# Attention of a hybrid streaming encoder on one Trainium2 core: chunks in pairs, unpadded queries, weight splits on one engine, one rescaling moved

## The chip, the cores and the metric

The kernel is one launch on one core of a Trainium2 chip. Five engines work side by side, each on its own queue of instructions: TensorE (PE in the profile) multiplies matrices into PSUM, VectorE (DVE) and ScalarE (ACT) read PSUM and SBUF, GpSimd (POOL) works on SBUF alone, and SyncE (SP) issues most of the transfers. The metric is the time of one execution on the device in microseconds, the median of several runs; lower is better.

## What is computed

The reference is one inference step of a two-layer encoder. 16 meta tokens and 256 new frames (the prompt) and 32 frames of a running stream (the sample) share all weights, so the kernel carries 304 tokens side by side. A layer is a half-step SwiGLU, a mixer and a second half-step SwiGLU, each between two RMS norms. Of the mixer this is the part that the change touches:

```python
s = jnp.einsum('bnqkgd,bnskd->bnkgqs', qb, kb).astype(jnp.float32) * ATTN_SCALE   # 64 ** -0.5
m = jnp.maximum(jnp.max(scores, axis=-1, keepdims=True), sink)
p = jnp.exp(scores - m)
return p / (jnp.sum(p, axis=-1, keepdims=True) + jnp.exp(sink - m))
```

There are 8 query heads in 2 groups, each group with one key and value head of 64 channels, and one learned sink per head. The prompt is attended in 4 chunks of 64 queries; a chunk sees up to 192 keys. The sample sees 128 cached keys and its own 32, the meta tokens see themselves. Beside the attention the mixer has 8 retention heads, a gate and an output projection.

## The kernel before

Activations lie transposed: channels on partitions, the 304 tokens along the free axis. Every large product is written by `mm3` as three products of rounded fp32 parts (L233, L234 and L236: weight high by input high, weight low by input high, weight high by input low). A weight piece of 128x512 arrives by DMA (`raw`), ACT rounds it to `hi` (L182), and a subtraction makes `lo` (L185); `split_one` does both. The pieces are split up to 8 ahead of their use. One piece feeds 12 matmuls. While a mixer's projection runs, every second subtraction goes to POOL (`POOLN = 2`), otherwise all go to DVE.

The order of the work is fixed when the program is written. `group4` and `group2` emit matmuls and call `tick`, which moves a counter on (775 for 6 matmuls of a `group2`). Side work waits in the lists `later`, `A` (attention) and `R` (retention) with a due count, and is emitted between the matmuls when the counter passes it; so it stands in each engine's queue at that place, whatever the clock says. `START`, `D_UNIT`, `D_NORM`, `D_TRANS`, `D_PV`, `KT` and `VT` are such counts: the start of a head group's attention, the distance of its units, and the offsets of normalising, transposing and of the product with the values.

The mixer computes the projection in this order: keys, values and queries of head group 0 (`group4`), queries of head group 1, then twice rotary keys, rotary queries and retention values, then two gates (`group2` each), and behind `flush` and `gate_out` the output projection in two `group4` of 8 pieces. `done_q` scales the queries with the norm's factor `rb` into `qb`. A unit of attention is one chunk of one head group: its stationary operand is 128 channels by 128 columns, in which one head of each pair fills the upper 64 rows and the other the lower 64, with zeros elsewhere, so that two matmuls (L981) give the scores of 4 heads. `softmax` reduces (L957), takes the sink in with two small operations (L958, L959), lets ACT exponentiate (L961); `norm` adds the sink's term (L966), inverts (L967) and scales on ACT (L968) and DVE (L969). Then PE transposes (L991), ACT (L999) and DVE (L997) copy out, and PE multiplies with the values (L1009). `side_unit` does the same for the sample and the meta tokens (L1032, L1033, L1030, L1042, L1056). PE transposes the scaled values once (L928, in the list under `VT`).

The residual `x` is kept multiplied by a norm's deviation after each sub-layer; `Post.unscale` undoes that, with a reciprocal on DVE (L539) and 8 products on POOL (L541). It stands in the mixer ahead of the second rotary queries and in a feed-forward layer at its third pair of output columns. `Post.done0` and `done1` take the output projection's results out of PSUM: ACT squares (L480, L493), POOL adds the squares of the first half (L483).

## Time and profile before

| | |
|---|---|
| median of 3 runs | 1239.14 us (1237.02 to 1241.27) |
| the profiled execution | 1237.22 us, its span 1235.4 us |
| granted TensorE clock, mean of the span | 0.987 |
| busy share of the span | PE 96%, PE weight load 93%, DVE 67%, ACT 48%, POOL 21% |
| bytes moved | 182.52 MB, 148 GB/s |

The profile was taken in one execution. Its time is 1.9 us under the median of the three runs and 1.8 us longer than its span. The two mixers lie at about 252 to 390 us and 859 to 990 us of the span. A busy share is a mean over stages with different limits.

### The profile page before, as it was taken

To read this page: it belongs to the slowest core of one execution; us is meant where nothing else is said; L and a number is where in the kernel's file an instruction comes from. 1 tells how busy PE (TensorE), PEld (TensorE's weight loads), DVE (VectorE), ACT (ScalarE), POOL (GpSimd) and SP (SyncE) were. 2 spreads that over 40 slices of the span, in tenths; PEclk is the share of its full clock that TensorE was granted. 3 is DMA by queue.
4 is the path that set the end of the run, shared out by engine and by line. 5 is a ranking of instruction groups with operands and counts; after the bars stand their busy time and mean duration, and the time that the engine had idled before them with its cause. 6 is when DMAs were issued, how large, how long until landed. Compare 5 with 4: busy or idle time off the path is not lost. (4 is left out here: it accounts for less than half of the span.)

```text
span 1235.4 us, 22814 instructions
## 1 busy us (share of the span) xinstructions
PE 1187.0 (96%) x8650; PEld 1153.7 (93%) x8650; DVE 828.3 (67%) x1501; ACT 596.2 (48%) x1226; POOL 254.1 (21%) x254
## 2 busy tenths in 40 slices
PE   8999999999999999999999999998999998999995
PEld 8999999897899999999999999998878988999995
DVE  7676654587767886564498656457875777766543
ACT  6454544455445545444355444344544553555442
POOL 4200001263625320001032000015435262000000
PEclk9999999999999999999999999999999999999998
DMA  7765455443233564554435554553533525645531
GB/s 226 164 183 159 139 190 165 157 143 111 83 109 120 154 188 144 169 181 145 148 98 176 159 176 144 183 159 122 167 96 113 154 65 175 196 147 161 193 108 39
DMA packets 155310, 182.52 MB, mean 148 GB/s; under 512 B 12016, under 2 KB 125984, under 8 KB 154944
## 3 DMA queue, kind: packets, MB, share of 16 engines
q1 hardware_dynamic: 153488, 178.84, 46.9%
q0 software_dynamic: 1344, 1.76, 1.0%
q8 instruction: 68, 1.11, 0.4%
q10 hardware_dynamic: 368, 0.47, 0.1%
q14 instruction: 42, 0.34, 0.1%
HBM read 175.70 MB, written 2.23 MB: 144 GB/s over the span
## 5 line engine op out<-in xcount | busy, mean ns | idle before, releaser
L233 PE MATMUL bk<-act,hi 128*128 128x304 f32 (+1 forms) x1824 | 559.8, 309 | 14.5 <-DVE act L516 6.5
L234 PE MATMUL bk<-act,lo 128*128 128x304 f32 (+1 forms) x1824 | 546.9, 302 | 0.6 <-DVE lo L185 0.6
L236 PE MATMUL bk<-act,hi 128*128 128x304 f32 (+1 forms) x1824 | 526.0, 303 | 4.0 <-DVE act L396 3.6
L185 DVE TENSOR_TENSOR lo<-raw,hi 128x512 fp32r<-128x512 f32 x604 | 416.0, 732 | 139.3 <-ACT hi L182 135.9
L182 ACT ACTIVATE hi<-raw 128x512 fp32r<-128x512 f32 x647 | 369.1, 621 | 148.6 <-PE bk L236 123.4
L233 PEld LDWEIGHTS bk<-act,hi 128*128 128x128 f32 x1824 | 345.9, 190 | 23.0 <-DVE act L516 8.0
L234 PEld LDWEIGHTS bk<-act,lo 128*128 128x128 f32 x1824 | 346.2, 190 | 2.1 <-DVE lo L185 1.1
L236 PEld LDWEIGHTS bk<-act,hi 128*128 128x128 f32 x1824 | 338.6, 190 | 7.2 <-DVE act L396 7.1
L233 PE MATMUL bk<-hh,hi 128*128 128x304 f32 (+1 forms) x704 | 210.4, 300 | 0.0
L234 PE MATMUL bk<-hh,lo 128*128 128x304 f32 (+1 forms) x704 | 210.1, 299 | 0.0
L236 PE MATMUL bk<-hl,hi 128*128 128x304 f32 (+1 forms) x704 | 207.9, 301 | 0.0
L483 POOL TENSOR_TENSOR acc<-acc,sq 128x304 f32<-128x304 f32 (+1 forms) x18 | 16.1, 894 | 577.7 <-ACT sq L480 576.5
L563 ACT ACTIVATE sg<-tg 128x304 f32<-128x304 f32 (+1 forms) x88 | 40.0, 455 | 192.1 <-DVE tg L562 190.8
L233 PEld LDWEIGHTS bk<-hh,hi 128*128 128x128 f32 x704 | 132.6, 188 | 0.0
L234 PEld LDWEIGHTS bk<-hh,lo 128*128 128x128 f32 x704 | 132.3, 188 | 0.0
L236 PEld LDWEIGHTS bk<-hl,hi 128*128 128x128 f32 x704 | 131.0, 188 | 0.0
L562 DVE TENSOR_TENSOR tg<-bk,rb 128x304 f32<-128x304 f32 (+1 forms) x88 | 40.9, 465 | 71.4 <-PE bk L236 71.3
L566 ACT ACTIVATE hh<-tu 128x304 fp32r<-128x304 f32 (+1 forms) x88 | 40.0, 455 | 68.8 <-DVE tu L565 68.8
L567 DVE TENSOR_TENSOR hl<-tu,hh 128x304 fp32r<-128x304 f32 (+1 forms) x88 | 41.6, 472 | 46.0 <-ACT hh L566 46.0
L185 POOL TENSOR_TENSOR lo<-raw,hi 128x512 fp32r<-128x512 f32 x44 | 59.2, 1356 | 46.4 <-ACT hi L182 46.4
L515 POOL TENSOR_TENSOR x<-x,s 128x304 f32<-128x304 f32 (+1 forms) x35 | 31.3, 927 | 130.8 <-ACT s L507 130.8
L541 POOL TENSOR_TENSOR x<-x,rs 128x304 f32<-128x304 f32 (+1 forms) x40 | 41.0, 1062 | 77.9 <-DVE rs L539 64.4
(238 smaller groups left out, 937.0 us busy)
## 6 DMA issues: line engine op xcount, KB each, us to landing
raw<-in_ffn_w_in_dram SPq DMA_DIRECT2D x352, 256.0 KB, 4.6
raw<-in_ffn_w_out_dram SPq DMA_DIRECT2D x88, 512.0 KB, 4.7
raw<-in_w_in_dram SPq DMA_DIRECT2D x36, 512.0 KB, 3.9
raw<-in_w_out_dram SPq DMA_DIRECT2D x16, 512.0 KB, 3.9
raw<-in_w_in_dram SPq DMA_DIRECT2D x16, 256.0 KB, 3.0
dec<-in_dec_dram SPq DMA_DIRECT2D x2, 1280.0 KB, 7.1
t<-t SPq DMA_DIRECT2D x24, 76.0 KB, 2.2
out_dram<-xgm SPq DMA_DIRECT2D x2, 384.0 KB, 3.5
```

The lines of the kernel that those rows point to most:

```text
L182: ACT.activation(out=hi, in_=r, func=ACTF.Copy)
L185: (POOL if i and st["pool"] and i % st["pool"] == 0 else DVE).tensor_tensor(out=lo, in0=r, in1=hi.bitcast(F32), op=ALU.subtract)
L233: PE.matmul(out=out, lhsT=a, rhs=xh, start=first, stop=False)
L234: PE.matmul(out=out, lhsT=b, rhs=xh, start=False, stop=False)
L236: PE.matmul(out=out, lhsT=a, rhs=xl, start=False, stop=last)
L483: POOL.tensor_tensor(out=self.acc[:, T0:], in0=self.acc[:, T0:], in1=sq[:, T0:], op=ALU.add)
L515: POOL.tensor_tensor(out=x[:, j, T0:], in0=x[:, j, T0:], in1=self.s[:, T0:], op=ALU.mult)
L541: POOL.tensor_tensor(out=x[:, k, T0:], in0=x[:, k, T0:], in1=rs[:, T0:], op=ALU.mult)
L562: DVE.tensor_tensor(out=tg[:, T0:], in0=bk[j][:, :n], in1=rb[:, T0:], op=ALU.mult)
L563: ACT.activation(out=sg[:, T0:], in_=tg[:, T0:], func=ACTF.Silu)
L566: ACT.activation(out=hh[a][:, T0:], in_=tu[:, T0:], func=ACTF.Copy)
L567: DVE.tensor_tensor(out=hl[a][:, T0:], in0=tu[:, T0:], in1=hh[a][:, T0:].bitcast(F32), op=ALU.subtract)
```

## The change

It does four things. (1) Queries are kept unpadded (`qa`): a head's 64 channels stand on the 64 rows of its half, scaled by -1/8, and the score matmul of each half uses 64 rows of the array, with the two halves in two PSUM banks. Two neighbouring chunks make one unit (`attn_pair`). The same holds for the sample and the meta tokens. (2) The negated sink is copied as one more column beside the scores in PSUM, so that the minimum, the exponentials and their sum take it in; the two small operations, the sink's own exponential and the addition go. (3) All subtractions of the weight splits run on DVE. (4) `unscale` of the mixer is emitted early in its output projection, and that of the feed-forward layers ahead of their output projection; the last layer keeps its place. The due counts are changed with it.

```diff
-POOLN = 2
...
-START = (12613, 11713)
-D_UNIT = 1987
-D_NORM = 1188
-D_TRANS = 3200
-D_PV = 5574
-KT = 7700
-VT = 5787
+START = (11000, 11713)
+D_UNIT = 4100
+D_NORM = 2800
+D_TRANS = 6500
+D_PV = 9300
+KT = 10500
+VT = 8500
...
+UNSCALE = 3000
...
-        (POOL if i and st["pool"] and i % st["pool"] == 0 else DVE).tensor_tensor(out=lo, in0=r, in1=hi.bitcast(F32), op=ALU.subtract)
+        DVE.tensor_tensor(out=lo, in0=r, in1=hi.bitcast(F32), op=ALU.subtract)
...
-                if g == 2 and prev:
+                if g == 2 and prev and last:
                     prev.unscale()
...
+            if prev and not last:
+                later.append((clock[0] + UNSCALE, prev.unscale))
...
-        qb = tl("qb", [P, 2, 2, 4, 2, CH])
-        qs = tl("qs", [P, 2, 2, 2, DEC])
-        POOL.memset(qb, 0.0)
-        POOL.memset(qs, 0.0)
-        qm = None
-        if not lastl:
-            qm = tl("qm", [P, 2, 2, 2, NMETA])
-            POOL.memset(qm, 0.0)
+        qa = tl("qa", [P, 2, 4, 2, CH])
...
-                for par in range(2):
-                    s = slice(64 * par, 64 * par + 64)
-                    DVE.tensor_tensor(out=qb[s, g, m, :, par], in0=y[s, NMETA - o:SA - o].rearrange("p (c t) -> p c t", c=4),
-                                      in1=rb[s, NMETA:SA].rearrange("p (c t) -> p c t", c=4), op=ALU.mult)
-                    DVE.tensor_tensor(out=qs[s, g, par, m], in0=y[s, SA - o:N - o], in1=rb[s, SA:N], op=ALU.mult)
-                    if qm is not None:
-                        DVE.tensor_tensor(out=qm[s, g, par, m], in0=y[s, 0:NMETA], in1=rb[s, 0:NMETA], op=ALU.mult)
+
+                def scaled(out, a, e):
+                    DVE.scalar_tensor_tensor(out=out, in0=y[:, a - o:e - o], scalar=-0.125, in1=rb[:, a:e], op0=ALU.mult,
+                                             op1=ALU.mult)
+                DVE.scalar_tensor_tensor(out=qa[:, g, :, m], in0=y[:, NMETA - o:SA - o].rearrange("p (c t) -> p c t", c=4),
+                                         scalar=-0.125, in1=rb[:, NMETA:SA].rearrange("p (c t) -> p c t", c=4),
+                                         op0=ALU.mult, op1=ALU.mult)
...
-        def softmax(S, rows, nk, nb, sink, nsink):
...
-            DVE.tensor_reduce(out=mx, in_=S, axis=AXX, op=ALU.max)
-            DVE.scalar_tensor_tensor(out=nm, in0=mx, scalar=-0.125, in1=nsink, op0=ALU.mult, op1=ALU.min)
-            DVE.tensor_tensor(out=es, in0=nm, in1=sink, op=ALU.add)
-            for j in range(nb):
-                ACT.activation(out=pt[r, j, 0:nk], in_=S[:, j], func=ACTF.Exp, scale=0.125, bias=nm[:, j:j + 1],
-                               accum_out=dn[:, j:j + 1])
-            ACT.activation(out=es, in_=es, func=ACTF.Exp)
...
+        K0 = 16
+
+        def softmax(parts, rows):
+
+            pt = tl("pt", [P, 2, 2, 208], bufs=2)
+            sm = tl("sm", [P, 3, 2, 2], bufs=2)
+            r, np_ = slice(0, rows), len(parts)
+            for a, (S, nk, sink) in enumerate(parts):
+                DVE.tensor_copy(S[:, :, K0 - 1:K0], sink.rearrange("p (b o) -> p b o", o=1))
+                for b in ([slice(0, 2)] if nk[0] == nk[1] else [slice(0, 1), slice(1, 2)]):
+                    DVE.tensor_reduce(out=sm[r, 0, a, b], in_=S[:, b, K0 - 1:K0 + nk[b.start]], axis=AXX, op=ALU.min)
+                for b in range(2):
+                    e = slice(K0 - 1, K0 + nk[b])
+                    ACT.activation(out=pt[r, a, b, e], in_=S[:, b, e], func=ACTF.Exp, scale=-1.0, bias=sm[r, 0, a, b:b + 1],
+                                   accum_out=sm[r, 1, a, b:b + 1])
 
             def norm():
-                DVE.tensor_tensor(out=dn, in0=dn, in1=es, op=ALU.add)
-                DVE.reciprocal(out=rd, in_=dn)
-                ACT.activation(out=pt[r, 0, 0:nk], in_=pt[r, 0, 0:nk], func=ACTF.Copy, scale=rd[:, 0:1])
-                DVE.tensor_scalar(out=pt[r, 1, 0:nk], in0=pt[r, 1, 0:nk], scalar1=rd[:, 1:2], scalar2=None, op0=ALU.mult)
+                DVE.reciprocal(out=sm[r, 2, 0:np_], in_=sm[r, 1, 0:np_])
+                for a in range(np_):
+                    for b in range(2):
+                        w = pt[r, a, b, K0:K0 + parts[a][1][b]]
+                        rd = sm[r, 2, a, b:b + 1]
+                        if (a if np_ > 1 else b) == 0:
+                            ACT.activation(out=w, in_=w, func=ACTF.Copy, scale=rd)
+                        else:
+                            DVE.tensor_scalar(out=w, in0=w, scalar1=rd, scalar2=None, op0=ALU.mult)
...
+        def attn_pair(g, c0):
+
+            cs = (c0, c0 + 1)
+            nk = [WIN[c][1] - WIN[c][0] for c in cs]
...
-                b = bank()
-                v = b.rearrange("p (j n) -> p j n", j=2)
-                for j in range(2):
-                    PE.matmul(out=v[:, j, 0:nk], lhsT=qb[:, g, j, c - 1].rearrange("p a t -> p (a t)"), rhs=kd[:, g, k0:k1],
-                              start=True, stop=True)
-                e["pt"], e["norm"] = softmax(v[:, :, 0:nk], P, nk, 2, sinkP[:, 2 * g:2 * g + 2], ia[0][:, 2 * g:2 * g + 2])
+                bs = [bank() for _ in range(2)]
+                for u, c in enumerate(cs):
+                    for par in range(2):
+                        s = slice(64 * par, 64 * par + 64)
+                        PE.matmul(out=bs[par][:, 256 * u + K0:256 * u + K0 + nk[u]],
+                                  lhsT=qa[s, g, c - 1].rearrange("p j t -> p (j t)"), rhs=kd[s, g, WIN[c][0]:WIN[c][1]],
+                                  start=True, stop=True)
+                parts = [(bs[par].rearrange("p (u n) -> p u n", u=2), nk,
+                          nsinkp[:, l, g, par:par + 1].to_broadcast([P, 2])) for par in range(2)]
+                e["pt"], e["norm"] = softmax(parts, P)
...
+                pT = tl("pT", [P, 2, 2, 2, P], bufs=2)
+                bs = [bank() for _ in range(2)]
+                for u, c in enumerate(cs):
+                    o = K0
+                    for i, (nm, n) in enumerate(PIECES[c]):
+                        for par in range(2):
+                            PE.transpose(out=bs[u][0:n, (2 * i + par) * P:(2 * i + par + 1) * P],
+                                         in_=e["pt"][:, par, u, o:o + n], identity=ident)
...
             def pv():
-                if c == 1:
-                    obk.append(bank())
-                ob = obk[0].rearrange("p (j t) -> p j t", j=2)
-                np_ = len(PIECES[c])
-                for i, (nm, n) in enumerate(PIECES[c]):
+                ob = bank()[:, 0:4 * CH].rearrange("p (j c t) -> p j c t", j=2, c=2)
+                todo = [(u, i, nm, n) for u, c in enumerate(cs) for i, (nm, n) in enumerate(PIECES[c])]
+                todo.sort(key=lambda x_: x_[3] <= 64)
+                for w, (u, i, nm, n) in enumerate(todo):
                     for par in range(2):
-                        PE.matmul(out=ob[64 * par:64 * par + 64, :, (c - 1) * CH:c * CH],
-                                  lhsT=vpc[nm][0:n, g * HD:g * HD + HD],
-                                  rhs=e["pT"][0:n, i, :, 64 * par:64 * par + 64], start=i == 0, stop=i == np_ - 1)
-                if c == 4:
-                    dh, dl = ah[:, 2 * g:2 * g + 2, NMETA:SA], al[:, 2 * g:2 * g + 2, NMETA:SA]
-                    ACT.activation(out=dh, in_=ob, func=ACTF.Copy)
-                    DVE.tensor_tensor(out=dl, in0=ob, in1=dh.bitcast(F32), op=ALU.subtract)
+                        PE.matmul(out=ob[64 * par:64 * par + 64, :, u], lhsT=vpc[nm][0:n, g * HD:g * HD + HD],
+                                  rhs=e["pT"][0:n, u, i, par].rearrange("p (j t) -> p j t", j=2), start=w == 0,
+                                  stop=w == len(todo) - 1)
+                a = NMETA + (c0 - 1) * CH
+                dh, dl = (t[:, 2 * g:2 * g + 2, a:a + 2 * CH].rearrange("p j (c t) -> p j c t", c=2) for t in (ah, al))
+                ACT.activation(out=dh, in_=ob, func=ACTF.Copy)
+                DVE.tensor_tensor(out=dl, in0=ob, in1=dh.bitcast(F32), op=ALU.subtract)
...
                 for g in range(2):
-                    w = q[:, g].rearrange("p a b t -> p (a b t)")
-                    if meta:
-                        PE.matmul(out=v[0:rows, g, 0:nk], lhsT=w, rhs=kd[:, g, 0:NMETA], start=True, stop=True)
-                    else:
-                        PE.matmul(out=v[0:rows, g, 0:P], lhsT=w, rhs=kc[:, g], start=True, stop=True)
-                        PE.matmul(out=v[0:rows, g, P:nk], lhsT=w, rhs=kd[:, g, SA:N], start=True, stop=True)
-                e["pt"], e["norm"] = softmax(v[0:rows, :, 0:nk], rows, nk, 2, sink, nsink)
+                    for o, k in ((0, kd[:, :, 0:NMETA]),) if meta else ((0, kc), (P, kd[:, :, SA:N])):
+                        for par in range(2):
+                            s = slice(64 * par, 64 * par + 64)
+                            k_ = k[s, g]
+                            PE.matmul(out=v[2 * n * par:2 * n * par + 2 * n, g, K0 + o:K0 + o + k_.shape[1]],
+                                      lhsT=q[s, g].rearrange("p j t -> p (j t)"), rhs=k_, start=True, stop=True)
+                e["pt"], e["norm"] = softmax([(v[0:rows], (nk, nk), sink)], rows)
...
-                for g in range(2):
-                    for par in range(2):
-                        for i, (o, m) in enumerate(pcs):
-                            src = vpc["E"] if meta else (cv.rearrange("p g d -> p (g d)") if i == 0 else vpc["S"])
+                for i, (o, m) in enumerate(pcs):
+                    src = vpc["E"] if meta else (cv.rearrange("p g d -> p (g d)") if i == 0 else vpc["S"])
+                    for g in range(2):
+                        for par in range(2):
                             PE.matmul(out=ob[64 * par:64 * par + 64, 2 * g:2 * g + 2],
                                       lhsT=src[0:m, g * HD:g * HD + HD],
-                                      rhs=e["pT"][0:m, i, g, 2 * n * par:2 * n * par + 2 * n], start=i == 0,
-                                      stop=i == len(pcs) - 1)
+                                      rhs=e["pT"][0:m, i, g, 2 * n * par:2 * n * par + 2 * n], start=i == 0 and g == 0,
+                                      stop=i == len(pcs) - 1 and g == 1)
...
-            obk = []
-            us = [attn_unit(g, c, obk) for c in (1, 2, 3, 4)]
...
-            if i == 1:
-                prev.unscale()
...
         flush()
-        st['pool'] = 0
         gate_out()
+        later.append((clock[0] + UNSCALE, prev.unscale))
```

`side_unit` scores per half as well. Where the change moves instructions, three places are shown in the order of the built program, without times. The first is DVE at the start of the first mixer, from the splits behind the norm to the scaled values (`sd`, `rb`: the norm's factor; `zk`, `kd`: keys; `zv`: values). Before:

```order
L185 TENSOR_TENSOR lo<-raw,hi 128x512 x3
L458 SCALAR_TENSOR_TENSOR sd<-bk,se 128x304
L461 RECIPROCAL rb<-sd 128x304
L185 TENSOR_TENSOR lo<-raw,hi 128x512
L897 TENSOR_TENSOR zk<-bk,rb 128x304
L900 TENSOR_TENSOR kd<-bk,rb 64x304 x2
L920 TENSOR_TENSOR zv<-bk,rb 128x304
```

The same place of the changed program:

```order
L185 TENSOR_TENSOR lo<-raw,hi 128x512 x6
L458 SCALAR_TENSOR_TENSOR sd<-bk,se 128x304
L461 RECIPROCAL rb<-sd 128x304
L185 TENSOR_TENSOR lo<-raw,hi 128x512 x2
L892 TENSOR_TENSOR zk<-bk,rb 128x304
L895 TENSOR_TENSOR kd<-bk,rb 64x304 x2
L915 TENSOR_TENSOR zv<-bk,rb 128x304
```

Four splits that stood on POOL stand on DVE ahead of the scaled values. On PE the transposes of these values stood 54 large matmuls behind the norm's sum and now stand 72 behind it.

The second place is POOL from the end of the first mixer's projection to the next norm (`osb`: retention output; `acc`: the sum of squares). Before:

```order
L890 TENSOR_TENSOR osb<-osb,gsd 128x304
L185 TENSOR_TENSOR lo<-raw,hi 128x512
L890 TENSOR_TENSOR osb<-osb,gsd 128x304
L483 TENSOR_TENSOR acc<-acc,sq 128x304 x3
L489 TENSOR_SCALAR xg<-x,gcol 128x304
L515 TENSOR_TENSOR x<-x,s 128x304 x7
```

The same place of the changed program:

```order
L885 TENSOR_TENSOR osb<-osb,gsd 128x304 x3
L541 TENSOR_TENSOR x<-x,rs 128x304 x8
L483 TENSOR_TENSOR acc<-acc,sq 128x304 x3
L489 TENSOR_SCALAR xg<-x,gcol 128x304
L515 TENSOR_TENSOR x<-x,s 128x304 x7
```

The 8 products of `unscale` now stand ahead of the sums of squares.

The third place is ACT in the same output projection, whose order stays but whose fourth row (the last square of the first half) goes into a buffer that the first of POOL's sums must have read. In the changed program:

```order
L480 ACTIVATE sq_4519<-bk_4369 128x304
L480 ACTIVATE sq_4529<-bk_4370 128x304
L182 ACTIVATE hi_4533<-raw_4328 128x512
L182 ACTIVATE hi_4537<-raw_4328 128x512
L1138 ACT_TABLE_LOAD
```

So that square stands behind the 8 products, and the roundings of the weight pieces behind it.

## Rows read from the trace of the kernel before

**Rows 1.** The page: busy time by engine with its share, and instructions.

```profile
PE 1187.0 (96%) x8650; PEld 1153.7 (93%) x8650; DVE 828.3 (67%) x1501; ACT 596.2 (48%) x1226; POOL 254.1 (21%) x254
```

**Rows 2.** Waits of PE over the span: total us, times, longest us.

```profile
PE bk L991 <- ACT pt L968: 4.2, 5, 1.6
PE bk L928 <- DVE zv L920: 2.8, 2, 1.6
PE bk L1042 <- ACT pt L968: 2.4, 2, 1.2
```

**Rows 3.** One stretch: length, busy PE, PEld, DVE, ACT, POOL, granted clock.

```profile
252.00:300.00 48.00, 44.11 (x320) 40.82 (x322) 41.02 (x96) 26.82 (x81) 23.19 (x19) 1.00 0.49 141
```

**Rows 4.** Groups by line on DVE and POOL, 252 to 300 us.

```profile
L185 DVE TENSOR_TENSOR lo<-raw,hi 128x512 fp32r<-128x512 f32 x12 | 12.9, 1098 | 3.5 <-ACT hi L182 3.4
L958 DVE SCALAR_TENSOR_TENSOR sm<-sm,nsinkp 128x2 f32<-128x2 f32 x7 | 4.0, 564 | 0.2
L957 DVE TENSOR_REDUCE sm<-bk 128x2 f32<-128x384 f32 (+2 forms) x7 | 3.2, 452 | 0.0
L185 POOL TENSOR_TENSOR lo<-raw,hi 128x512 fp32r<-128x512 f32 x12 | 16.4, 1381 | 5.8 <-ACT hi L182 5.7
```

**Rows 5.** DVE in order of time: start, length, instructions, two places.

```profile
252.90 4.95 DVE L185 TENSOR_TENSOR lo<-raw,hi 128x512 fp32r<-128x512 f32 x3 [0.15 <-ACT hi L182]
373.81 4.65 DVE L185 TENSOR_TENSOR lo<-raw,hi 128x512 fp32r<-128x512 f32 x7
430.38 6.87 DVE L185 TENSOR_TENSOR lo<-raw,hi 128x512 fp32r<-128x512 f32 x6
```

**Rows 6.** PE in order of time: start, length, three insertions and the matmuls around them.

```profile
281.41 0.30 PE L234 MATMUL bk<-act,lo 128*128 128x304 f32 x1
281.55 0.30 PE L236 MATMUL bk<-act,hi 128*128 128x304 f32 x1
281.78 0.44 PE L1009 MATMUL bk<-pT,vpE 80*64 80x128 f32 x4
282.15 0.41 PE L233 MATMUL bk<-act,hi 128*128 128x304 f32 x1
282.39 0.30 PE L234 MATMUL bk<-act,lo 128*128 128x304 f32 x1
...
277.64 0.81 PE L981 MATMUL bk<-kd,qb 128*128 128x192 f32 x4
278.15 0.44 PE L233 MATMUL bk<-act,hi 128*128 128x304 f32 x1
...
337.36 1.13 PE L834 MATMUL bk<-qr,kr 64*128 64x272 f32 x12
338.42 0.41 PE L233 MATMUL bk<-act,hi 128*128 128x304 f32 x1
```

**Rows 7.** PE in order of time: the sample's products with the values.

```profile
325.00 0.33 PE L1056 MATMUL bk<-pT,cv 128*64 128x64 f32 x2
327.05 0.40 PE L233 MATMUL bk<-act,hi 128*128 128x304 f32 x1
```

**Rows 8.** ACT by line, 238 to 360 us.

```profile
L961 ACT ACTIVATE pt<-bk,sm 128x192 f32<-128x192 f32 (+4 forms) x20 | 7.4, 372 | 19.0 <-DVE sm L958 18.5 <-PE bk L991 0.5
L961 ACT ACTIVATION_READ_ACCUMULATOR pt<-bk,sm 128x1 f32 (+1 forms) x20 | 3.9, 196 | 0.0
```

**Rows 9.** DVE, POOL and ACT in order of time, four places; last, a group of DVE.

```profile
365.24 0.47 DVE L1099 TENSOR_TENSOR act<-osb,act 128x304 fp32r<-128x304 f32 x1 [0.52 <-ACT act L1098]
...
430.55 9.27 POOL L541 TENSOR_TENSOR x<-x,rs 128x304 f32<-128x304 f32 x8 [15.04 <-DVE rs L539]
...
370.68 3.07 POOL L483 TENSOR_TENSOR acc<-acc,sq 128x304 f32<-128x304 f32 x3 [11.11 <-ACT sq L480]
...
371.92 0.42 ACT L480 ACTIVATE sq<-bk 128x304 f32<-128x304 f32 x1 [0.41 <-PE bk L236]
...
L539 DVE RECIPROCAL rs<-s 128x304 f32<-128x304 f32 (+1 forms) x5 | 10.1, 2024 | 0.0
```

More of the change, by code (lines that the diff above doesn't have):

```diff
@@ L156, in tile_hybrid_step @@
     raws, split = {}, {}
-    st = {"dma": 0, "split": 0, "use": 0, "free": 0, "cap": 1 << 30, "pool": 0, "ramp": 0}
+    st = {"dma": 0, "split": 0, "use": 0, "free": 0, "cap": 1 << 30, "ramp": 0}
     def load_to(c, between=lambda: None):
@@ L376, in late_loads @@
             POOL.dma_start(out=t, in_=I[nm])
-        for par in range(2):
-            POOL.dma_start(out=sinkp[64 * par:64 * par + 64], in_=sink_ap(par, [[0, 64], [8, DEPTH], [2, 4]]))
+        for j in range(2):
+            POOL.dma_start(out=sinkp[64 * j:64 * j + 64], in_=sink_ap(2 * j, [[0, 64], [8, DEPTH], [4, 2], [1, 2]]))
         for b, h0 in enumerate((0, 2, 1, 3)):
@@ new lines, in scores @@
+                e["pt"], e["norm"] = softmax(parts, P)
+            def trans():
+                pT = tl("pT", [P, 2, 2, 2, P], bufs=2)
[6 more added lines that the diff above has]
+                                         in_=e["pt"][:, par, u, o:o + n], identity=ident)
+                        o += n
+                for u, c in enumerate(cs):
+                    for i, (nm, n) in enumerate(PIECES[c]):
+                        src = bs[u][0:n, 2 * i * P:(2 * i + 2) * P].rearrange("p (a t) -> p a t", a=2)
+                        if i:
+                            DVE.tensor_copy(pT[0:n, u, i], src)
+                        else:
+                            ACT.activation(out=pT[0:n, u, i], in_=src, func=ACTF.Copy)
@@ L1016, in attn_unit, with side_unit @@
+                ACT.activation(out=dh, in_=ob, func=ACTF.Copy)
+                DVE.tensor_tensor(out=dl, in0=ob, in1=dh.bitcast(F32), op=ALU.subtract)
             return scores, trans, pv, lambda: e["norm"]()
-        def side_unit(q, n, t0, sink, nsink, meta):
+        def side_unit(q, n, t0, sink, meta):
             e = {}
```

46 lines of the change are left out of this document (13 added, 33 removed).

## The prediction

> **What bounds the kernel now.** I read the page first: PE is busy 1187.0 us [rows 1] of a span of 1235.4 us. Its share, 96%, leaves little, so an edit gains only where PE stands still or where PE's own work becomes shorter. Next I read PE's waits. In the attention PE waits 4.2 us for probabilities that are not scaled yet when their transposes stand next in its queue, 2.4 us for the same in the sample's unit, and 2.8 us for the scaled values: 9.4 us over both mixers [rows 2]. The reader is to see that all three come through DVE and ACT. PE's other waits lie in code that stays.
>
> Why they are late shows in the table of a stretch and its groups. From 252 to 300 us DVE is busy 41.0 us of 48, and POOL 23.2 us [rows 3]. Twelve subtractions of the weight splits take 1.10 us each on DVE there and twelve 1.38 us on POOL [rows 4]. Where POOL is idle seven take 4.65 us, so 0.66 us each; three beside POOL's splits take 4.95 us, 1.65 each [rows 5]. Both slow each other when they run side by side, and the short reductions of the softmax stand behind them in DVE's queue.
>
> **The splits on DVE.** In this stretch DVE gets 12 more subtractions: 12 x 0.66 = 7.9 us. Its own 12 may fall from 1.10 to 0.66: -5.2 us. That gives 43.7 us of 48, below 100% but not less than before; I count no gain from the edit by itself. What falls besides is the work with the sink: an operation of 2 elements took 0.56 us [rows 4], and two of these per unit become one small copy per half of a pair.
>
> **The chain in pairs.** The counts give the time that a chain may take. 775 counts are 6 matmuls, and one matmul of the projection follows another after 0.14 us (281.41 to 281.55) [rows 6]. Before, 3200 counts between scores and transposes are 25 matmuls, 3.5 us. After, 6500 are 50, so 7.0 us, and with the insertions of other work between them rather 8.2 (an estimate: six short insertions of 0.2). What must happen in it: two reductions of 0.45 and two copies not longer, together at most 1.8 us [rows 4]; four exponentials of 0.37 + 0.20 us, 2.3 us [rows 8], the first beside the second reduction; an inversion and the scalings, some 0.8. That is 4.5 us, against some 3.4 before for one chunk (0.45, two small operations of 0.56, 1.1 of exponentials, 0.8). So the slack of nearly nothing becomes 2.5 to 3.7 us. DVE's queue may still hold two splits and four products in front; that is what the slack is for. The transposes of the values come 18 matmuls (2.5 us) later, while DVE gets four more splits ahead of them (2.6 us, partly given back by the faster ones): their longest wait of 1.6 us should fall too. Pairs take longer until the products with the values, between transposes and products 2800 counts give 22 matmuls, 3.1 us, for four copies on ACT and DVE where two stood in 2.6 us; there I expect some 2.0 us of new, small waits over both layers. **Waits: -9.4 + 2.0 = -7.4 us; bounds 0 and -9.4.**
>
> **PE's own work.** An insertion costs more than its columns. In front of four products with the values PE takes 0.23 us from start to start instead of 0.14 (281.55 to 281.78), and behind them 0.24 (282.15 to 282.39) [rows 6]: 0.09 + 0.10 us per insertion. Scores of two chunks of 192 keys took 0.51 us each (277.64 to 278.15) and some 0.14 of coming back, 1.30 us. The 64-row form does not occur in the attention before, but the retention's scores have it: two halves with 272, 144 and 48 columns, 464 each, took 1.06 us (337.36 to 338.42) [rows 6]. For 384 columns per half that is 0.88, with entry and return 1.08: 8 pairs save 8 x 0.22 = 1.8 us; I put 1.6. The Trainium skill, "TensorEngine Tiling (Array Packing)", section "Theoretical Speedup", gives up to twice the speed where the contraction has 64 rows or fewer; by it the two halves would take half of the 1.02 us, and the pairs would save 3.5 to 4 us instead of 1.6. Its section "Key Properties" says that a change of the tiling mode drains the engine, which speaks against short insertions of this form; the 0.09 us above are what the rows show of such a change. I go by the retention's rows.
>
> Products with the values: 16 insertions become 8, 8 x 0.19 = 1.5 us. Transposes: eight returns fewer, 0.8 us. The sample's products with the values alternate between 128 and 32 rows and take 2.05 us for 8 (325.00 to 327.05) [rows 7], 0.26 each; grouped by form they should come near 0.15, so 0.8 us per layer, 1.6. The sample's and the meta tokens' scores change their form three times and may cost 0.6. **PE's work: -1.6 - 1.5 - 0.8 - 1.6 + 0.6 = -4.9 us; bounds -2 and -8** (none of the changes of form given back, or all of them and parallel halves).
>
> **The moved `unscale`.** At the mixer's old place it held DVE for one inversion of 2.0 us [rows 9] and POOL beside the attention; that these are gone there is part of the waits above. At the new place its inversion stands behind the gates and two splits on DVE: the last gate product ends at 365.24 + 0.47 = 365.7, two splits 1.3, the inversion 2.0: 369.0 us. Eight products beside DVE's splits took 9.27 us [rows 9] while six of those splits took 6.87 [rows 5]: 378.3. The first sum of squares, about 1.0 us of POOL (three took 3.07), then frees the buffer that ACT's last square needs: 379.3 instead of 371.9, 7.4 us late [rows 9], and ACT's roundings of the next pieces are queued behind it. PE has six pieces ahead there, 6 x 12 x 0.14 = 10.1 us, so PE should not wait; if the cover were gone, the whole 7.4 per layer would be paid, 14.8. I take 0.5 per layer for a late split. In the feed-forward layers the inversion goes to a stretch of 22 splits where DVE has little else, and POOL has nothing until the first square: 0. The memsets that go and the second copy of the outputs (one per pair) lie beside POOL's and ACT's idle time: 0. **+1.0 us; bounds 0 and 14.8.**
>
> **Sum.** The profiled execution took 1237.2 us, 1.9 below the median of the runs: 1237.2 - 7.4 - 4.9 + 1.0 = 1225.9. Runs scatter upwards of it, so I say **1226.5 us**. A main case without one of the smaller terms lies between 1222 and 1231.
>
> **Rivals.**
> - *The waits only move.* DVE has as much to do as before (43.7 of 48), so the same 9.4 us come back in front of the products with the values or at the scaled values. 1237.2 - 4.9 + 1.0 = 1233.3 us. For it speaks that DVE's load does not fall; against it the slack, twice as long for a chain that is a third longer. Chance 0.16.
> - *The output group collides.* `unscale` delays ACT by 7.4 us in each mixer, and the cover of 10.1 us is not there, because the pieces behind are rounded late. It decides where fewer than 5 pieces are ready. 1237.2 - 7.4 - 4.9 + 14.8 = 1239.7, no change. In the Trainium skill, "SBUF — State Buffer", section "Who interferes with whom", DVE with two SBUF inputs and POOL share a port pair, and the one that comes second blocks fully; the 9.27 us of the eight products and the 6.87 of the six splits beside them (4.0 where POOL is idle) agree with it. By this rule moving all splits off POOL is right and putting the products beside splits is wrong. Chance 0.10.
> - *The pairs come late: slower.* The chain of 4.5 us stands behind four rotary products (1.8 us), three splits (2.0) and ACT's roundings (0.6 each, three) in the queues. If that exceeds some 8.2 us, all of PE waits, for two chunks at once: eight pairs, late by 2 us each, cost 16: 1237.2 - 4.9 + 1.0 + 16 = 1249. For it speaks DVE at 90% there, against it that no wait longer than 1.6 us is seen now [rows 2]. Chance 0.08.
> - *More falls than I count.* All 9.4 us go, and PE's work falls by the far bound: 1237.2 - 9.4 - 8 = 1219.8 us. It needs halves that run side by side, and the rows of the retention speak against that. Chance 0.16.
>
> **How the numbers follow.** The main case has 0.50. Main case, first rival and the last one hold 0.82; a little at each end for scatter gives 1217 to 1239. A change of 0.3% (3.7 us) is about what can be told from none. Faster than 1235.4: the main case, the last rival, and most of the first: 0.78. Same: the rest of the first and most of the second: 0.13. Slower: the third and a rest of the second: 0.09.
>
> **What would show the steps.** In the changed profile PE's waits for the transposes (now L1003 and L1054) and for the values (L923) should be under 3 us together, and new ones in front of L1021 and L1068 under 2. DVE's subtractions between 252 and 300 us should take 0.66 to 0.70 us, and none stand on POOL. The sum of PE's time between the first and the last matmul of a mixer should fall by 5 to 7 us per layer. ACT's fourth square (L480) in the output projection should wait for POOL some 4 to 7 us, and PE's L234 behind it not at all. I would be wrong where PE waits at L1003 or L1021 more than before, where DVE's splits remain at 1.1 us without POOL, or where the 64-row scores take over 1.3 us a pair.

## The result and the profile after

The changed kernel takes 1223.19 us, median of 4 runs (1221.81 to 1223.71); the ratio to the kernel before is 0.9869, 95% interval 0.985 to 0.9888. The profiled execution took 1221.81 us with a span of 1220.0 us, 15.4 less than before. Run once more beside the experiments, the same kernel stood at 0.9874 (0.9853 to 0.9895).

The head of the changed kernel's page answers to [rows 1]: PE has 8.7 us less work and waits less, POOL 58 us less, and DVE does not have more although it took all 44 splits of POOL.

```profile
span 1220.0 us, 22701 instructions
PE 1178.3 (97%) x8670; PEld 1149.0 (94%) x8670; DVE 820.9 (67%) x1491; ACT 593.6 (49%) x1211; POOL 195.6 (16%) x205
```

The waits of PE in the changed kernel answer to [rows 2] (total us, times, longest):

```profile
PE bk L233 <- DVE act L516: 6.5, 3, 2.2
...
PE bk L233 <- ACT hi L182: 3.5, 1, 3.5
...
PE bk L233 <- DVE dec L777: 2.2, 4, 0.8
PE bk L1021 <- ACT pT L1012: 2.0, 4, 0.6
...
PE bk L1021 <- DVE pT L1010: 0.7, 2, 0.3
```

No row is left for the transposes of the probabilities, for the sample's or for the scaled values. Two waits are new: 2.7 us in front of the products with the values (the last two rows), and 2.2 us in the output projections for the decayed keys (L777). The first two rows shown stood before as well, outside the mixers. The second of them is one matmul of the last feed-forward layer, which no edit below touches, and it changes all the same: 3.6 us before, 3.5 here, 3.2 when run again, and from nothing to 5.5 us in the other runs. Two kernels whose times are 2 us apart may differ by it alone.

The same stretch of the first mixer, 252 to 300 us, answers to [rows 3, 4]; the DVE groups stand under the window:

```profile
252.00:300.00 48.00, 46.66 (x370) 42.55 (x370) 39.60 (x99) 29.32 (x89) 7.07 (x7) 1.00 0.53 152
...
L185 DVE TENSOR_TENSOR lo<-raw,hi 128x512 fp32r<-128x512 f32 x25 | 17.4, 738 | 5.2 <-ACT hi L182 5.2
L958 DVE COPY bk<-nsinkp 128x2 f32<-128x2 f32 x8 | 1.2, 155 | 0.0
```

PE runs 370 matmuls in it where 320 ran. A split takes 0.74 us on DVE instead of 1.10, but DVE stands idle 5.2 us in front of its 25 splits whose rounding ACT has not done (3.5 us in front of 12 before).

PE in order of time shows the three insertions whose price was predicted: the scores of a pair, the sample's products with the values, and a pair's products with the values (start, length).

```profile
273.30 0.30 PE L236 MATMUL bk<-act,hi 128*128 128x304 f32 x1
273.53 0.92 PE L989 MATMUL bk<-kd,qa 64*128 64x192 f32 x8
274.38 0.41 PE L233 MATMUL bk<-act,hi 128*128 128x304 f32 x1
...
313.40 0.45 PE L1068 MATMUL bk<-pT,cv 128*64 128x64 f32 x8
313.78 0.45 PE L1068 MATMUL bk<-pT,vpS 32*64 32x64 f32 x8
314.15 0.78 PE L881 MATMUL bk<-sq,blk 128*128 128x304 f32 x2
...
281.74 0.30 PE L236 MATMUL bk<-act,hi 128*128 128x304 f32 x1
282.57 0.71 PE L1021 MATMUL bk<-pT,vpE 80*64 80x128 f32 x8 [0.53 <-ACT pT L1012]
```

From start to start a pair's scores take 0.23 + 0.85 us; the sample's products 0.75 us where they took 2.05 [rows 7]; and PE reaches the products of the first pair 0.5 us before their copies are done.

A gain that PE's list of waits had not announced lies in the retention's scores. In the kernel before, the second of them looked like this; the last line is from the list of waits of the weight load (PEld):

```profile
306.85 0.44 PE L1009 MATMUL bk<-pT,vpF 64*64 64x128 f32 x4
307.22 1.95 PE L834 MATMUL bk<-qr,kr 64*128 64x272 f32 x12
309.10 0.41 PE L233 MATMUL bk<-act,hi 128*128 128x304 f32 x1
...
PEld bk L834 <- ACT vt L822: 1.0, 2, 0.5
```

It took 1.88 us where the same twelve records take 1.06 elsewhere [rows 6]. One half runs from 307.22; the other starts at 308.04 only, 0.05 us after ACT has copied the retention's transposed values (`vt`) out of PSUM. That copy stands on ACT behind exponentials that waited 3.10 us for DVE:

```profile
306.12 0.42 ACT L961 ACTIVATE pt<-bk,sm 128x192 f32<-128x192 f32 x1 [3.10 <-DVE sm L958]
...
307.50 0.49 ACT L822 ACTIVATE vt<-bk 128x384 f32<-128x384 f32 x1
```

Records of PE's first half fill most of that time, so PE's list of waits is silent; only the weight load's list has the wait, with two times 0.5 us. The other mixer has the same (1.82 for 1.03). In the changed kernel all eight take 1.03 to 1.06: 1.6 us gained.

The output group of the first mixer in the changed kernel, DVE, POOL, ACT and PE:

```profile
357.95 2.05 DVE L539 RECIPROCAL rs<-s 128x304 f32<-128x304 f32 x1
359.91 0.69 DVE L777 TENSOR_TENSOR dec<-bk,kdec 128x384 f32<-128x384 f32 x2
...
360.07 8.30 POOL L541 TENSOR_TENSOR x<-x,rs 128x304 f32<-128x304 f32 x8 [9.54 <-DVE rs L539]
...
369.21 0.42 ACT L480 ACTIVATE sq<-bk 128x304 f32<-128x304 f32 x1 [6.74 <-POOL acc L483]
...
364.81 0.38 PE L233 MATMUL bk<-ah,hi 128*128 128x304 f32 x1 [0.75 <-DVE dec L777]
```

ACT's last square waits 6.7 us for POOL, and no piece is late for it. PE waits for something else: `dec` reads four PSUM banks that the second half of the projection wants, and the inversion of `unscale` stands ahead of it on DVE.

### The profile page after: what moved, and what is told of

The parts are those of the page before. It is cut to its first block, busy times and chain, and to the rows that moved or that the text cites. A ratio compares the mean times of both kernels' runs of the same rounds, so it can differ in the third digit from the quotient of the medians.

```text
span 1220.0 us, 22701 instructions
## 1 busy us (share of the span) xinstructions
PE 1178.3 (97%) x8670; PEld 1149.0 (94%) x8670; DVE 820.9 (67%) x1491; ACT 593.6 (49%) x1211; POOL 195.6 (16%) x205
## 5 line engine op out<-in xcount | busy, mean ns | idle before, releaser
L185 DVE TENSOR_TENSOR lo<-raw,hi 128x512 fp32r<-128x512 f32 x648 | 440.3, 726 | 135.2 <-ACT hi L182 132.0
L541 POOL TENSOR_TENSOR x<-x,rs 128x304 f32<-128x304 f32 (+1 forms) x40 | 45.2, 1162 | 319.0 <-DVE rs L539 319.0
L564 DVE TENSOR_TENSOR tu<-bk,rb 128x304 f32<-128x304 f32 (+1 forms) x88 | 40.9, 465 | 20.4 <-PE bk L236 11.4
L565 DVE TENSOR_TENSOR tu<-tu,sg 128x304 f32<-128x304 f32 (+1 forms) x88 | 42.4, 482 | 14.7 <-ACT sg L563 10.1
```

Of the source, the lines that this page charges most:

```text
L185: DVE.tensor_tensor(out=lo, in0=r, in1=hi.bitcast(F32), op=ALU.subtract)
L541: POOL.tensor_tensor(out=x[:, k, T0:], in0=x[:, k, T0:], in1=rs[:, T0:], op=ALU.mult)
L564: DVE.tensor_tensor(out=tu[:, T0:], in0=bk[2 + j][:, :n], in1=rb[:, T0:], op=ALU.mult)
L565: DVE.tensor_tensor(out=tu[:, T0:], in0=tu[:, T0:], in1=sg[:, T0:], op=ALU.mult)
```

## The experiments

Ratios are to the kernel before on the same chip, with 95% intervals. The runs were made in four sets, and runs of different sets are compared by ratio.

**All splits on DVE, in the kernel before.**

```diff
-POOLN = 2
+POOLN = 0
```

> The kernel before, with all subtractions of the weight splits on DVE and nothing else changed. Theory A (the waits in the attention come from chains that have too few counts, 25 matmuls for a chain of 3.4 us): most of the 9.4 us of waits of rows 2 stay, at least 6 us, and the time falls by 0 to 3 us, to 1236-1239. Theory B (they come from DVE and POOL slowing each other): DVE's subtractions fall from 1.10 to about 0.7 us between 252 and 300 us, under 3 us of the waits remain, and the time falls by 6 us or more, under 1233.

Measured: 1247.93 us, ratio 1.0092 (1.0077 to 1.0107): slower by 11 us. Both forecasts of the time fall. Of theory A it holds that the waits stay. Of theory B it holds that DVE's splits become short (median 0.69 us), and yet the waits grow. PE's waits, and DVE and ACT in order of time in this run:

```profile
PE bk L233 <- ACT hi L182: 5.4, 1, 5.4
PE bk L991 <- ACT pt L968: 5.1, 4, 2.0
...
PE bk L928 <- DVE zv L920: 3.6, 2, 2.0
...
PE bk L886 <- ACT sq L881: 2.0, 1, 2.0
...
277.63 0.69 DVE L185 TENSOR_TENSOR lo<-raw,hi 128x512 fp32r<-128x512 f32 x1 [1.27 <-ACT hi L182]
278.24 0.15 DVE L966 TENSOR_TENSOR sm<-sm 128x2 f32<-128x2 f32 x1
278.43 0.17 DVE L967 RECIPROCAL sm<-sm 128x2 f32<-128x2 f32 x1
...
278.69 0.36 ACT L968 ACTIVATE pt<-pt,sm 128x80 f32<-128x80 f32 x1 [1.09 <-DVE sm L967]
```

DVE stands 1.27 us in front of a split that ACT has not rounded, and the softmax's three small operations (0.15 to 0.3 us each) are queued behind it; then ACT waits 1.09 us for them. A split on POOL that waits for its rounding blocks nobody's softmax. That is a third theory, C: the cost of a split on DVE is not its 0.66 us but the order in which two engines wait for each other.

Not all of the 11 us is shown to be that. The profiled span is 8.3 us longer than before (1243.7 us). The waits inside the two mixers grow by 3.9 us. Another 2.5 us of waits came at the start and in the last feed-forward layer, which the edit does not touch. The mean granted clock is 0.984 instead of 0.987, which is some 3 to 4 us more (an estimate from the two means); three stretches at 0.50 (1.2 of 2.4 GHz) lie in the projections of the mixers, where the kernel before has one. Whether the edit brought these on was not tried.

**POOL's splits restored in the changed kernel.** Theory C is tried from the other side.

```diff
-        DVE.tensor_tensor(out=lo, in0=r, in1=hi.bitcast(F32), op=ALU.subtract)
+        (POOL if i and i % 2 == 0 and st.get('pool') else DVE).tensor_tensor(out=lo, in0=r, in1=hi.bitcast(F32), op=ALU.subtract)
...
+        st['pool'] = 2
         first = group4(KD, xh, xl, N, (2, 3, 0, 1), lambda m, bk: stats() if m == 0 else None, lead=2)
...
         flush()
+        st['pool'] = 0
         gate_out()
```

> The changed kernel, with every second subtraction of a mixer's projection on POOL again. Theory A: the longer counts cover the slower DVE, the time rises by 0 to 3 us over the changed kernel (1223-1226), and waits for transposes and values stay under 2 us. Theory B: DVE's subtractions are at 1.1 us again, the waits come back, +5 us or more (over 1228).

Measured: 1218.63 us, ratio 0.9855 (0.9839 to 0.9872), profiled span 1216.5. It is not 5 us slower, as theory B would have it, nor up to 3 us slower, as theory A allowed, but if anything faster than the changed kernel (0.9869 and 0.9874; the intervals overlap). The profile is clearer than the times: both rows of waits in front of the products with the values, 2.7 us, are gone, though DVE's splits are long again:

```profile
L185 DVE TENSOR_TENSOR lo<-raw,hi 128x512 fp32r<-128x512 f32 x13 | 15.1, 1179 | 2.1 <-ACT hi L182 2.0
...
281.98 0.66 PE L1021 MATMUL bk<-pT,vpE 80*64 80x128 f32 x8
```

So the length of DVE's splits, on which the prediction had looked, did not matter. What fits is DVE's idle time in front of them: 2.1 us in front of 13 splits against 5.2 in front of 25. At the first pair's products the chain can be followed. DVE, ACT and ACT in the changed kernel, then DVE and ACT with POOL's splits:

```profile
278.64 0.69 DVE L185 TENSOR_TENSOR lo<-raw,hi 128x512 fp32r<-128x512 f32 x1 [1.70 <-ACT hi L182]
...
280.29 0.33 ACT L963 ACTIVATE pt<-bk,sm 128x81 f32<-128x81 f32 x1 [1.68 <-DVE bk L958]
...
282.14 0.65 ACT L1012 ACTIVATE pT<-bk 80x256 f32<-80x256 f32 x2
...
277.88 0.16 DVE L958 COPY bk<-nsinkp 128x2 f32<-128x2 f32 x1 [1.42 <-PE bk L989]
...
281.49 0.65 ACT L1012 ACTIVATE pT<-bk 80x256 f32<-80x256 f32 x2
```

In the changed kernel DVE stands 1.70 us in front of an unrounded split. The sink's copies and reductions of the next pair come late behind it, ACT's exponentials wait 1.68 us for them, and the copy of the transposed probabilities, queued behind these on ACT, starts at 282.14. With that split on POOL nothing stands in front of the sink's copy, and the copy of the probabilities starts at 281.49. Four such places take PE 1.99, 2.42, 2.08 and 2.48 us in the changed kernel, from the large matmul before the products to the one behind, and 1.33, 1.45, 1.32 and 1.40 us here. That is 3.5 us, of which the list of waits has 2.7, and as much as the spans differ (1220.0 and 1216.5). So theory C is shown at the first place, and the four places account for the difference.

**`unscale` at its old places.** The lines that move it are undone.

> The changed kernel, with unscale at its old places in the mixers and the feed-forward layers. If the new place costs what the changed profile shows (PE waits 2.2 us in the output projections for the decayed keys, which stand behind unscale's inversion on DVE) and the old place costs nothing now that the chains have slack, the time falls by 1 to 2.5 us (1221-1222). If the old place is what delayed the attention before (2.0 us of DVE and eight products on POOL beside it), 2 to 4 us of waits come back in front of the sample's transposes or the products with the values, and the time rises by 0 to 2 us.

Measured: 1219.73 us, ratio 0.9864 (0.985 to 0.9879). The waits for `dec` are gone, as expected; those in front of the products with the values stay (2.3 + 0.7 us), and the wait in the last feed-forward layer is 5.1 instead of 3.5 us. The time cannot be told from that of the changed kernel; PE's time by stage, at the end of this section, can.

**Padded queries in pairs.** The prompt's operand has 128 rows with zeros again. Of the edit the score matmul is shown; the operand `qa` is also cleared on POOL and written half by half.

```diff
-                                  lhsT=qa[s, g, c - 1].rearrange("p j t -> p (j t)"), rhs=kd[s, g, WIN[c][0]:WIN[c][1]],
+                                  lhsT=qa[:, g, c - 1, par].rearrange("p j t -> p (j t)"), rhs=kd[:, g, WIN[c][0]:WIN[c][1]],
```

> The changed kernel, with the prompt's queries padded again to 128 rows with zeros (pairs, sink column and the sample's scores as in the changed kernel). By the slots of the changed profile a pair with 192 keys takes 0.85 us and 0.23 in front; padded, eight records of 0.13 us make 1.03 and 0.14 in front: +0.1 us a pair, so +0.5 to +1 us in all with the way back into the projection. By the prediction's term (1.6 us for unpadded scores, pairing apart) +1.6 us. If halves on row tiles ran twice as fast, +3.5 us or more.

Measured: 1221.23 us, ratio 0.9875 (0.986 to 0.989), which cannot be told from the changed kernel. The time is no guide here, because other things moved with it: the wait of 3.5 us in the last feed-forward layer is absent, and 3.9 us instead of 2.7 are waited in front of the products with the values. The slots of PE can tell. PE around the same pair:

```profile
273.66 0.30 PE L236 MATMUL bk<-act,hi 128*128 128x304 f32 x1
273.80 1.46 PE L992 MATMUL bk<-kd,qa 128*128 128x192 f32 x8
274.96 0.44 PE L233 MATMUL bk<-act,hi 128*128 128x304 f32 x1
```

0.14 + 1.16 us against 0.23 + 0.85 for the 64-row form: 0.22 us a pair. The other four pairs have shorter windows and differ by 0.98 - 0.90 = 0.08. Over eight that is 4 x 0.22 + 4 x 0.08 = 1.2 us, where the prediction had 1.6. The Trainium skill, "TensorEngine Tiling (Array Packing)", section "Theoretical Speedup", gives up to a factor of two where a dimension is 64 or less. Here the score products became 1.16 / 0.85 = 1.36 times as fast, and the change of form in front costs 0.09 us.

**The counts alone, in the kernel before.**

```diff
-START = (12613, 11713)
-D_UNIT = 1987
-D_NORM = 1188
-D_TRANS = 3200
-D_PV = 5574
+START = (11000, 11713)
+D_UNIT = 2050
+D_NORM = 2800
+D_TRANS = 6500
+D_PV = 9300
```

`KT` and `VT` are set to the new values too.

> The kernel before with single chunks, padded queries and half of the splits on POOL, and only the due counts lengthened to those of the change (START 11000, D_NORM 2800, D_TRANS 6500, D_PV 9300, KT 10500, VT 8500; distance of units 2050). If the waits vanish because a chain has twice the counts, rows 2's 9.4 us fall under 2 us and with the 1.6 us hidden in the retention's scores the time falls by 6 to 10 us (ratio 0.992 to 0.995). If pairs or the shorter softmax are needed for it, at least 5 us of waits stay and the ratio is 0.997 to 1.000.

Measured: 1232.6 us, ratio 0.9957 (0.9943 to 0.9972). PE's waits of this run that remain in the attention:

```profile
PE bk L1009 <- ACT pT L999: 3.7, 2, 1.9
...
PE bk L991 <- DVE t L749: 1.5, 2, 1.1
```

Some 0.6 us more wait for the retention's DVE work. So 5.8 us of waits remain of 9.4, most of them behind the transposes, and the ratio lies between the two forecasts: longer counts alone bring a third of the gain.

**The pairs with the old offsets.** `D_NORM`, `D_TRANS` and `D_PV` back to 1188, 3200 and 5574; `START`, `D_UNIT`, `KT` and `VT` stay as changed.

> The changed kernel with the offsets of before inside a unit (D_NORM 1188, D_TRANS 3200, D_PV 5574); pairs, unpadded queries and the sink column stay. A pair's chain then has 25 matmuls (3.5 us) for some 4.5 us of work. If the counts are what took the waits away, each pair and each side unit waits 1 to 2 us at its transposes (L1003, L1054): 8 to 18 us of waits, the time 1230 to 1240. If pairs with fewer small operations suffice, under 4 us of waits and the time under 1226.

Measured: 1225.09 us, ratio 0.9905 (0.9891 to 0.992), some 0.3 to 0.4% above the changed kernel. The interval lies above that kernel's first one and overlaps its second. The waits are between the two forecasts, and so is the cause:

```profile
PE bk L1003 <- ACT pt L973: 5.9, 6, 1.5
```

Pairs with short offsets keep 5.9 us of waits, and yet about three quarters of the gain: what they bring lies mostly in PE's own work. The projections of the mixers are 14.8 us shorter than before (189.0 instead of 203.8), and only 3.8 of these are listed waits. Whether fewer operations of the softmax or fewer, longer units did it was not taken apart.

**The keys' decay ahead of the inversion,** due at once behind the gates.

```diff
-            A.append((lambda p=p: k_decay(p), clock[0] + 2000, False))
+            A.append((lambda p=p: k_decay(p), clock[0], True))
```

> The changed kernel with the four decays of the keys (k_decay) due at once behind the gates, so that they stand ahead of unscale's inversion in DVE's queue. If the 2.2 us of waits for the decayed keys are the banks that these hold while DVE inverts, the waits are gone and the time falls by about 2 us against the changed kernel. If DVE's queue is only full there, the 2 us come back as waits for split pieces or for the keys' transposes, and the time is the same within 1 us.

Measured: 1227.36 us, ratio 0.9915 (0.9889 to 0.9941): slower by some 5 us, against both forecasts. The waits for `dec` are gone, as the first had it, but the inversion starts 1.9 us later, ACT's square waits 9.2 us instead of 6.7, and now the pieces behind it and the sum of squares are late (ACT, then PE):

```profile
370.96 0.42 ACT L480 ACTIVATE sq<-bk 128x304 f32<-128x304 f32 x1 [9.21 <-POOL acc L483]
...
373.36 0.41 PE L234 MATMUL bk<-act,lo 128*128 128x304 f32 x1 [0.98 <-DVE lo L185]
379.70 1.30 PE L501 MATMUL bk<-acc,ones 128*128 128x304 f32 x2 [2.08 <-DVE acc L495]
```

**`unscale` later,** `UNSCALE = 9000`.

> The changed kernel with UNSCALE 9000 instead of 3000: the eight products on POOL start about 6 us later in each output group. In the mixers ACT's last square then waits for POOL some 12 to 13 us instead of 6.7. If six pieces ahead (10.1 us) are the cover, PE waits 2 to 4 us for split pieces in each mixer (L234 or L233), less the 2.2 us of the decayed keys, which now stand ahead of the inversion: net +2 to +6 us. If the cover is deeper than that, the decayed keys' waits go and the time falls by 1 to 2 us.

Measured: 1230.12 us, ratio 0.994 (0.9919 to 0.9961): slower by some 8 us, more than the 2 to 6 expected, though the waits for `dec` are gone and the square waits 9.9 us instead of the 12 to 13 expected. A piece comes 0.59 and another 0.98 us late, and the sum again 2.08:

```profile
372.95 0.41 PE L233 MATMUL bk<-act,hi 128*128 128x304 f32 x1 [0.59 <-ACT hi L182]
374.34 0.41 PE L234 MATMUL bk<-act,lo 128*128 128x304 f32 x1 [0.98 <-DVE lo L185]
380.69 0.78 PE L501 MATMUL bk<-acc,ones 128*128 128x304 f32 x2 [2.08 <-DVE acc L495]
```

**The inversion early, the products in the output group.** The inversion is emitted ahead of the second rotary queries.

> The changed kernel with unscale's inversion on DVE emitted ahead of the second rotary queries (where the whole of unscale stood before) and the eight products on POOL left in the output group. DVE's queue in the output group loses 2.0 us: the decayed keys are in time (2.2 us of waits gone) and the products start about 2 us earlier, so ACT's last square waits some 4.5 us instead of 6.7. Expected 1.5 to 2.5 us faster than the changed kernel; if the inversion at the old place delays the attention, up to 2 us come back there.

Measured: 1223.46 us, ratio 0.9892 (0.9877 to 0.9907): no gain, against the expectation. Without the inversion to wait for, POOL starts its products at once, beside the gates, and DVE's gate products take 1.12 us instead of 0.47:

```profile
350.36 8.55 POOL L546 TENSOR_TENSOR x<-x,rs 128x304 f32<-128x304 f32 x8
...
350.88 1.12 DVE L1112 TENSOR_TENSOR osb<-osb,zg 128x304 f32<-128x304 f32 x1
...
PE bk L233 <- DVE dec L782: 3.0, 4, 0.8
```

The gates end some 2.5 us later, and `dec` starts at 360.5 us instead of 359.9 although no inversion stands ahead of it. The same with POOL's splits:

> As the run with the early inversion, and every second subtraction of the mixers' projection on POOL again. If the two gains are independent (about 2 us here, 2 to 3 us from the splits, whose waits lie in front of the products with the values), the ratio to before is 0.981 to 0.984, 1214 to 1217 us, better than both kernels. If the inversion beside POOL's splits costs the attention its slack, no better than the run with POOL's splits alone (0.9855).

Measured: 1220.15 us, ratio 0.9866 (0.985 to 0.9883), no better than POOL's splits alone. The wait in the last feed-forward layer is 2.2 us longer than there (5.5 against 3.3), which alone exceeds the difference.

**Pairs, unpadded queries, sink column and counts alone;** splits and `unscale` as in the kernel before.

> The first, second and counts parts of the change alone (pairs of chunks, unpadded queries, sink column, due counts); the splits and unscale as in the kernel before. If the two other parts cost or give nothing by themselves in this kernel, the ratio to before lies at that of the changed kernel with POOL's splits (0.9839 to 0.9872), and the 2.2 us of waits for the decayed keys are absent. If POOL with its splits and unscale together slows the attention again, waits of 2 to 4 us stand in front of the transposes or the products with the values and the ratio is 0.987 or above.

Measured: 1218.69 us, ratio 0.9845 (0.9816 to 0.9874). The waits for `dec` and for the products with the values are both absent; one wait of 2.6 us for POOL's rotary queries is new. So the whole gain belongs to parts (1) and (2) with their counts. By the times, parts (3) and (4) together cost 0.2 to 0.3% or nothing; the intervals overlap.

**The changed kernel again,** beside the runs with the counts, the keys' decay and the late `unscale`.

> The changed kernel unaltered, beside its variants on one chip: ratio to the kernel before of 0.985 to 0.989 as measured first.

Measured: 1221.91 us, ratio 0.9874 (0.9853 to 0.9895), with the same rows of waits (2.1 + 0.7 and 2.2 us). The three runs beside it are compared with this time.

**PE's time by stage.** The trace of each run gives the time from the first large matmul behind the norm's sum (L453) to the first of the output projection, and from there to the sum of squares (L501). Both are sums over the two mixers, in us; the last column counts stretches at a granted clock of 0.50 in the projections.

| | projections | output groups | at 0.50 |
|---|---|---|---|
| kernel before | 203.8 | 55.7 | 1 |
| changed kernel | 185.6 | 59.0 | 0 |
| POOL's splits restored | 182.1 | 59.0 | 0 |
| `unscale` at its old places | 187.5 | 55.7 | 1 |
| pairs, unpadded queries, sink column, counts alone | 186.2 | 55.7 | 1 |

One stretch costs some 1.7 us (an estimate: 3.4 us at half the clock). The projections became 18.2 us shorter. The new place of `unscale` costs 3.3 us in the output groups, and the old place cost next to nothing in the projections: 187.5 less 1.7 is 185.8. All splits on DVE cost 3.5 us. In the run without both, the wait for POOL's rotary queries, the stretch at the lower clock and 5.2 us of wait in the last feed-forward layer hide most of what that saves.

## Why the prediction was right, step by step

- **The waits, -9.4 + 2.0.** Right. All three rows are gone and 2.7 us came in front of the products with the values. The cause given for the old waits, DVE and POOL slowing each other, was wrong in part: with all splits on DVE and nothing else the waits in the mixers grow by 3.9 us. What took the waits away is the longer lead together with the pairs: the counts alone leave 5.8 us of waits and the pairs with the old offsets 5.9, both together 2.7, and with POOL's splits none.
- **The splits on DVE, 0.** The step that was mis-sized. I had worked with busy time (43.7 of 48 us expected, 39.6 measured) and saw neither gain nor loss. In the changed kernel the edit costs PE 3.5 us in the projections, which POOL's splits give back.
- **PE's work, -4.9.** Right in sign, low in size. The sample's products gave 2.6 us over both layers instead of 1.6. The unpadded scores gave 1.2 by the padded run; I had counted all eight pairs with 384 keys, and four have 80 + 144. The retention's scores, not in the sum at all, gave 1.6. The terms for the products' insertions, the transposes and the side scores were not tried one by one.
- **`unscale`, +1.0.** Too small: the output groups became 3.3 us longer, and of these 2.2 are in the list of waits. The late square of rival two is there: a forecast of 7.4 us, 6.7 measured, and no piece is late for it. Where the square waits 9.2 and 9.9 us, PE pays 3.1 and 3.7 us in the first mixer, so the cover was some 6 to 7 us (an estimate from these three runs) instead of 10.1; more than half of the price stands at the sum of squares, which I had not followed. The 2.2 us that PE does lose come with the inversion on DVE ahead of `dec`, whose banks I had not followed either: with `dec` ahead of the inversion they are gone.
- **The rest of the difference.** The sum for the profiled execution was 1225.9 us, it took 1221.81. In the projections the sum had 7.4 + 4.9 = 12.3 us less, and 18.2 were measured; in the output groups it had 1.0 us more, and 3.3 were measured. That the time lies so near the forecast is in part luck, because these two misses are of opposite sign. Of the 5.9 us in the projections the retention's scores are 1.6 and the sample's products 1.0, and 1.7 are the stretch at the lower clock that the kernel before has there and the changed one does not. It follows a wait of PE for the sample's transposes that is gone; whether it came of that wait or by chance was not tried. Against them stand 0.7 us more of listed waits than forecast in front of the products. The remaining 2 us or so I did not assign.
- **The signs.** Waits at the transposes and for the values are gone, as forecast. Those in front of the products are 2.7 us where under 2 was named. DVE's splits have a median of 0.69 us (0.66 to 0.70 named), a pair's scores stay at 1.08 us, under 1.3. PE's time in a mixer, projection and output group together, fell by 7.3 and 7.6 us, where 5 to 7 was named.
- **The rivals.** "The waits only move" holds for 2.7 + 2.2 us. "The pairs come late" did not come: with 25 instead of 50 matmuls of lead the pairs wait 5.9 us in all, and the kernel is still faster than before. "More falls than I count" comes nearest for the projections, but not for the reason that it named: the two halves did not take half the time (0.85 us against 1.16 padded).

## What to carry to other kernels

An instruction that must wait for another engine holds up everything queued behind it on its own engine: 1.70 us in front of one split became 1.68 us on ACT. Busy time does not show that; the idle time in front of the instruction, with its releaser, does. Before work is moved to the "faster" engine, ask what it will stand in front of while it waits. For a chain that is late, neither more lead alone nor fewer, longer units alone removed the waits here (5.8 and 5.9 us left); both together did. Compare kernels by the time of a stage as well as by the whole: 3.3 us lost in two output groups could not be seen in the total. And when a slow block is moved to a quiet place, follow each PSUM bank and buffer that its new neighbours hold.

## What was not expected of the hardware

- PE can lose 0.8 us without a row in its own list of waits: with two matmuls on row tiles of 64 one half runs while the other waits (1.88 us for twelve records instead of 1.06). The list of the weight load shows 0.5 us of it.
- POOL's products beside DVE's gate products stretch these from 0.47 to 1.12 us, the same as for the splits (0.66 to 1.15 us and more [rows 5]). The Trainium skill, "SBUF — State Buffer", section "Who interferes with whom", says that a DVE instruction with two SBUF inputs contends with a GpSimd instruction that reads SBUF. The runs agree for the gate products and the splits; the subtractions between these gate products (L1114), with two SBUF inputs as well, took 0.51 us instead of 0.48.
- The granted clock of TensorE is 0.50 (1.2 of 2.4 GHz) in single stretches at places that differ from kernel to kernel: from 923.2 to 926.6 us in the kernel before, from 996.6 to 1000.0 us in the changed one, at neither place in the run with padded queries. PE had been busy 3.8 of the 5 us ahead of the first and 3.2 of the 5 ahead of the second, and all through both. One such stretch is worth some 1.7 us (an estimate: half of 3.4), as much as one of the smaller terms here.
